# Four dense expert tiles on 512 columns instead of five on 640, and two tiles gathered early

## The chip, the cores and the metric

One Trainium2 chip, one of its cores. The metric is the device time of one execution in microseconds. Engines: PE is TensorE's matmul side, PEld its weight loads, DVE VectorE, ACT ScalarE, POOL GpSimd, SP SyncE, whose queue issues most transfers.

## The reference

One layer for a prompt of 1024 tokens and 32 sample rows (8 sequences of 4 tokens), all in float32:

```python
h = _rms(x, norm1_g) * (1.0 + sc1) + sh1
proj = h @ w_in
o_attn = _dilated_attn_prompt(q, k, v, rel_bias)        # or the same over a cache, for the sample rows
y_rwkv, s_fin, shift_new = _rwkv_mixer(proj[..., 3 * C_ATTN:], shift0, wkv0, ...)   # delta rule, a scan over time
x = x + g1 * (jnp.concatenate([o_attn, y_rwkv], axis=-1) @ w_out)
h2 = _rms(x, norm2_g) * (1.0 + sc2) + sh2
x = x + g2 * _peer(h2)

# _peer, per token: 8 heads, 16 of 16384 single-neuron experts each
s1, i1 = lax.top_k(s[:, :, 0], 16)
s2, i2 = lax.top_k(s[:, :, 1], 16)
top_s, pos = lax.top_k(cand, 16)                # cand: the 256 sums; eid: their experts
gate = jax.nn.softmax(top_s, axis=-1)
act = gelu(einsum('nd,nhkd->nhk', hb, expert_u[eid]))
out = einsum('nhk,nhkd->nd', gate * act, expert_v[eid])
```

So a token uses 128 of 16384 experts, each a row of expert_u and a row of expert_v of 1024 numbers.

## The kernel before, in words

The prompt is cut into eight tiles of 128 tokens, 0 to 7; the sample rows are tile NT. The expert sum of a tile is made in one of two ways.

*Gathered* (`gather_u`, `gather_v`, lines 1509 and 1524): for each of 128 picks POOL issues an indirect DMA that brings one row of expert_u for every token (128 rows of 4 KB into a tile `row`), DVE multiplies it with the token's h2 (held in two PSUM banks, `gh`) and sums; after Gelu and gate the same is done with expert_v, and DVE adds `row * co` to an accumulator in PSUM (`gh` or `ga`). Five `row` buffers go round (`NROW`), which also hold h2 and the operands of `finish`. A tile takes 256 gathers; the sample rows take 64.

*Dense* (`dense`, line 1615): all 16384 experts for the tokens of several tiles at once, in 128 blocks of 128 experts. `hidden(b)` loads u in two pieces of 256 KB, splits each into two float32r parts (ACT casts `uh`, POOL subtracts `ul`), and makes three products per block of channels into PSUM `d`; then ACT applies Gelu, DVE multiplies with the gates `g` loaded from DRAM, ACT and DVE split the product into `ch` and `cl`. `output` multiplies four blocks' `ch`, `cl` with `vh`, `vl` (v loaded and split likewise) and DVE adds the bank to `dacc`. The gates come from `spread_gates` (line 1553): per tile 256 small matmuls of one-hot factors (`oha` by POOL and ACT, `ohb` by DVE) into PSUM `sp`, copied to `stage` and written to `g_d` in four pieces of 2 MB.

Before the change tiles 0 to 4 are dense (640 columns, worked as two halves of 320) and tiles 5, 6, 7 and NT are gathered. The program has this order: norm, projection and the first two prompt quarters of the delta rule (`rwkv_prompt`), unchanged here; a front part (lines 1789 to 1875) with the last two quarters (`delta`), attention of tiles 2 to 5, the output projection and second norm (`front`), the routing scores (`scores`), the picks (`picks`, whose POOL instructions are `tq`) and the spreads (`spreads`), then sample rows and attention of tiles 6 and 7; then the dense experts, with the routing of tiles 6, 7 and NT (`routed`) and the gathers (`gather_all`) beside them.

`weave` puts such streams side by side: a rough meter of engine times decides which stream makes its next step, streams under `fill` only go along, and the others get a higher priority. The final order on each engine comes from the tile framework's scheduler when the program is built; on the chip each engine's queue runs strictly in that order and waits on semaphores. `until(x)` lets a stream idle until a tile is ready.

Of the kernel before, what the change touches and what calls it, by code (L numbers as in the profile page):

```python
# [11 lines left out]
FT = mybir.dt.float32  # L12
# [52 lines left out]
def _shape_constants():  # L65
# [20 lines left out]
    # relative bias along distance, from 1023 down  # L86
# [7 lines left out]
    # the sample rows' keys: 4 of every 16 far rows, the near ones, the new ones  # L94
# [35 lines left out]
class _Meter:  # L130
    """a rough count of the engines' time, by which streams of work are put side by side."""
# [43 lines left out]
class _Ring(dict):  # L175
    """tiles by number, made when first asked for."""
# [25 lines left out]
def tile_hybrid_step(ctx, tc, ins, outs):  # L202
# [27 lines left out]
    def split(src, hi, lo, eng=None):  # L230
        """src as a sum of two float32r parts."""
# [3 lines left out]
    def piece(pool, src, kn, eng, bufs, wbufs):  # L235
        """1024 columns of weights, of kn blocks of rows: as two float32r parts."""
# [6 lines left out]
    def mm3(out, l, r, first, last):  # L243
        """a product of split operands, to float32's accuracy; or of unsplit ones."""
# [9 lines left out]
    def rsqrt(pool, x, scale, bias, shape, name, floor=None):  # L254
        """1 / sqrt(scale * x + bias), with one Newton step behind the table."""
# [57 lines left out]
    def open_picked(es, name, tiles, ring=None):  # L313
        """the chosen experts of some tiles, and their gates."""
# [12 lines left out]
    def mod_rows(pool, seg, i, tag, n, bufs=1):  # L327
        """one of the six modulation vectors, a row for every token of tile i."""
# [16 lines left out]
    # ---------------------------------------------------------------- modulation, first norm  # L345
# [7 lines left out]
    def ada_rows(pa, pp, scT, r, bufs):  # L353
# [17 lines left out]
        if r == 2:  # L371
            # the second norm's weights times its scale
# [31 lines left out]
    def norm_rows(pa, tiles):  # L404
        """the rows of some tiles over their root mean square."""
# [16 lines left out]
    def norm_in(pa, pp, tiles, put):  # L422
        """first norm of some tiles, transposed: put(k, part) for the channels 128 k.. ."""
# [99 lines left out]
    # ---------------------------------------------------------------- the delta-rule heads  # L523
# [11 lines left out]
    def delta_consts(rc):  # L535
# [5 lines left out]
        # tiles that keep zeros where a block is empty  # L541
# [16 lines left out]
    def log_decay(pool, pp, lt, c0, n):  # L558
        """token-major logarithm of the decay."""
# [7 lines left out]
    def key_norms(pool, pp, sqk, n, nj):  # L567
        """1 / max(|kk|, 1e-12), token-major."""
# [8 lines left out]
    def spread(pool, pp, rn, p, n, nj):  # L577
        """the norms of a pair of heads over their columns, transposed."""
# [9 lines left out]
    def group_norm(pool, pp, y, n, bv, g, c0):  # L588
        """y token-major; normalised per head, the bonus and the gate put on, into columns c0.. of the mix."""
# [24 lines left out]
    def rwkv_prompt(pp, side, qs):  # L614
        """quarters of the prompt, 256 tokens each, in chunks of 64; heads go in two groups of four, side by side."""
        n = 256
        both = (0, 1)
        for qi in qs:
            t0 = 256 * qi
            with ExitStack() as es:  # L620
# [97 lines left out]
                with ExitStack() as e3:  # L718
# [14 lines left out]
                    # inverses of the 32-blocks: two partitions a block, for its even and its odd rows  # L733
# [30 lines left out]
                def chunk(j, gq, ych, py):  # L764
                    """two chunks of 64 tokens, four heads."""
# [41 lines left out]
                    # right-hand sides [A | M_ak V], then (I - M_ab)^-1 of them  # L807
# [1191 lines left out]
```

## Time and profile before

| | us |
|---|---|
| median of three runs | 3811.39 |
| lowest, highest | 3810.4, 3816.43 |
| span of the profiled execution, first to last instruction | 3802.4 |

The profiled execution's own time is given as its span; the runs' times also hold what lies before its first and after its last instruction. Busy shares of the span: PE 91%, DVE 76%, POOL 55%, ACT 38%. The kernel moves 981.58 MB. In the groups of rows below an instruction is named by output and inputs (`d<-h2T,uh`), buffer numbers left out; all carry line 196, the helper that records every operation, so they are told apart by their tiles. In the tables by window the columns are the window and its length, then busy time and instruction count of PE, PEld, DVE, ACT and POOL, then the granted TensorE clock, the mean busy share of the 16 DMA engines, and GB/s.

### The profile page before, as it was taken

The numbers are of one execution on the slowest core, as the hardware profiler recorded it, in microseconds if no ns is written. First come the engines' busy times: TensorE is split into PE (matmuls) and PEld (weight loads), VectorE is DVE, ScalarE is ACT, GpSimd is POOL, SyncE is SP. The second block draws the span as 40 slices with busy tenths as digits, with TensorE's granted clock in tenths as the row PEclk, the third lists the DMA queues.
The fourth block names the chain that finished last, engine by engine and source line by source line (L and its number), as shares of the span: only waits on it lengthen the run. The fifth ranks groups of instructions, "written<-read, shape, count | busy, mean of one in ns | idle before, by whom it ended". The sixth has DMA issues, their size and how long they took to land.

```text
span 3802.4 us, 57197 instructions
## 1 busy us (share of the span) xinstructions
PE 3473.4 (91%) x19618; PEld 2873.5 (76%) x19618; DVE 2899.8 (76%) x6059; ACT 1428.1 (38%) x3124; POOL 2107.3 (55%) x1842
## 2 busy tenths in 40 slices
PE   7999999789889888969999989999999999999998
PEld 3878678567768664547877879888887878788886
DVE  2655364588688566777878999888888888888898
ACT  5544344336766654542411322222222222222221
POOL 3232021015555356656655777677677767677775
PEclk8999999899999899989999999999999999999999
DMA  9643695553765667749988779999889898899998
GB/s 292 196 143 115 189 280 170 164 181 134 241 210 179 206 222 229 259 156 328 324 303 283 230 263 327 320 317 312 308 303 318 306 315 303 307 312 320 327 324 311
DMA packets 592528, 981.58 MB, mean 258 GB/s; under 512 B 78323, under 2 KB 354620, under 8 KB 589420
## 3 DMA queue, kind: packets, MB, share of 16 engines
q1 hardware_dynamic: 467788, 524.84, 43.1%
q0 software_dynamic: 124448, 453.08, 33.9%
q8 instruction: 155, 2.54, 0.3%
q14 instruction: 137, 1.12, 0.1%
HBM read 882.97 MB, written 94.78 MB: 257 GB/s over the span
## 4 chain that ended last, share of the span: by engine, by line
PE 36%; DVE 23%; DMA 19%; issue 11%; POOL 8%; ACT 3%; SPq 1%; POOLq 0%; DVEq 0%; ACTq 0%
PE at L196 10%; PE d L196 9%; DMA u<-in_uT 8%; PE rw L196 5%; PE pj L196 5%; POOL row L196 4%; PE rs L196 3%; DVE gh L196 3%; DVE act L196 2%; DVE row L196 2%; DVE cl L196 2%; PE sp L196 2%; DMA row<-in_expert_v,eid 2%; POOL vl L196 2%; POOL ul L196 2%
## 5 line engine op out<-in xcount | busy, mean ns | idle before, releaser
L196 PE MATMUL d<-h2T,uh 128*128 128x320 f32 x4096 | 908.1, 311 | 11.6 <-ACT h2T L196 7.0
L196 PEld LDWEIGHTS d<-h2T,uh 128*128 128x128 f32 x4096 | 689.7, 189 | 21.2 <-ACT h2T L196 7.3
L196 PE MATMUL d<-h2T,ul 128*128 128x320 f32 x2048 | 632.8, 310 | 0.3 <-POOL ul L196 0.3
L196 POOL DMA_INDIRECT row<-in_expert_u,eid x416 | 405.7, 975 | 264.3 <-DVE co L196 90.0
L196 PE MATMUL d<-vl,ch 128*128 128x512 f32 x1280 | 512.2, 401 | 43.6 <-POOL vl L196 43.6
L196 PE MATMUL d<-vh,ch 128*128 128x512 f32 x1280 | 486.4, 401 | 51.2 <-DVE dacc L196 26.9
L196 DVE CUSTOM_DVE_ANT_0 row<-row,gh 128x1024 f32<-128x1024 f32 x416 | 499.4, 1210 | 34.7 <-DMA row<-in_expert_u,eid 26.0
L196 POOL DMA_INDIRECT row<-in_expert_v,eid x416 | 406.4, 977 | 183.5 <-DVE gh L196 66.2
L196 PE MATMUL d<-vh,cl 128*128 128x512 f32 x1280 | 505.6, 396 | 0.8 <-DVE cl L196 0.7
L196 POOL TENSOR_SCALAR oha<-c_iota,tr 128x128 f32<-128x128 f32 x320 | 309.6, 974 | 310.8 <-PE sp L196 297.9
L196 POOL TENSOR_TENSOR ul<-u,uh 128x512 fp32r<-128x512 f32 x256 | 336.6, 1324 | 139.7 <-ACT uh L196 129.7
L196 ACT CAST vh<-v 128x512 fp32r<-128x512 f32 x256 | 157.5, 620 | 623.2 <-DMA v<-in_expert_v 447.9
L196 PEld LDWEIGHTS d<-h2T,ul 128*128 128x128 f32 x2048 | 386.2, 189 | 2.7 <-issue 1.6
L196 DVE SCALAR_TENSOR_TENSOR gh<-row,co,gh 128x1024 f32<-128x1024 f32 x285 | 364.9, 1280 | 27.7 <-DMA row<-in_expert_v,eid 26.0
L196 PEld LDWEIGHTS d<-vh,ch 128*128 128x128 f32 x1280 | 243.0, 191 | 129.8 <-DVE dacc L196 43.3
L196 DVE TENSOR_TENSOR act<-act,g 128x320 f32<-128x320 f32 x256 | 279.2, 1090 | 77.2 <-ACT act L196 72.8
L196 POOL TENSOR_TENSOR wl<-w,wh 128x1024 fp32r<-128x1024 f32 x50 | 122.5, 2453 | 388.7 <-ACT wh L196 353.9
L196 PEld LDWEIGHTS d<-vl,ch 128*128 128x128 f32 x1280 | 244.4, 191 | 112.0 <-POOL vl L196 62.1
L196 POOL TENSOR_TENSOR vl<-v,vh 128x512 fp32r<-128x512 f32 x224 | 289.5, 1301 | 34.7 <-ACT vh L196 30.3
L196 ACT CAST ch<-act 128x320 fp32r<-128x320 f32 x256 | 117.7, 460 | 495.4 <-DVE act L196 464.2
L196 PEld LDWEIGHTS d<-vh,cl 128*128 128x128 f32 x1280 | 244.9, 191 | 53.9 <-DVE cl L196 2.0
L196 ACT CAST uh<-u 128x512 fp32r<-128x512 f32 x256 | 154.0, 617 | 257.0 <-DMA u<-in_uT 166.2
(449 smaller groups left out, 6932.7 us busy)
## 6 DMA issues: line engine op xcount, KB each, us to landing
u<-in_uT SPq DMA_DIRECT2D x256, 256.0 KB
v<-in_expert_v SPq DMA_DIRECT2D x256, 256.0 KB
w<-wq_d SPq DMA_DIRECT2D x224, 256.0 KB
g_d<-stage SPq DMA_DIRECT2D x20, 2048.0 KB
g<-g_d SPq DMA_DIRECT2D x64, 640.0 KB
w<-in_w_in SPq DMA_DIRECT2D x75, 512.0 KB
w<-in_w_out SPq DMA_DIRECT2D x112, 256.0 KB
adaw<-in_ada_w SPq DMA_DIRECT2D x32, 512.0 KB
```

The lines of the kernel that those rows point to most:

```text
L196: return f(*a, **k)
```

## The change

Tiles 2 to 5 are dense, 512 columns in one piece; tiles 0 and 1 are gathered, from when they are picked. Gelu and product stay in the PSUM bank. The spreads of the four dense tiles move out of the delta-rule part into the part with the sample rows, where `rwkv_sample` and `attn_sample` now follow each other in one stream. `gather_all` goes along (`fill`) from the start of the front part. Attention of tiles 6 and 7 drops `wide` (second buffers of kT and vr). Removed comments are left out of the diff.

```diff
-    NDENSE = 640
+    NDENSE = 512
...
-            for h in range(2):
-                if b % 4 == 0:
-                    G_[h] = pa.tile([128, n // 64, 4, 32], FT, tag="g", name="g", bufs=3)
-                    sy.dma_start(G_[h], g_d[n // 64 * h:n // 64 * (h + 1), :, b:b + 4].rearrange("s e i t -> e s i t"))
-                cs = slice(h * n // 2, (h + 1) * n // 2)
-                ps = pp("d")
-                for k in range(KD):
-                    mm3(ps[:, :n // 2], (uh[:, k], ul[:, k]), [x[:, k, cs] for x in h2T], k == 0, k == KD - 1)
-                t = pa.tile([128, n // 2], FT, tag="act", name="act", bufs=2)
-                sc.activation(t, ps[:, :n // 2], AF.Gelu)
-                tv = t.rearrange("p (s t) -> p s t", t=32)
-                ve.tensor_tensor(tv, tv, G_[h][:, :, b % 4], op=OP.mult)
-                split(t, ch[:, cs], cl[:, cs])
+            if b % 4 == 0:
+                G_[0] = pa.tile([128, n // 32, 4, 32], FT, tag="g", name="g", bufs=2)
+                sy.dma_start(G_[0], g_d[:, :, b:b + 4].rearrange("s e i t -> e s i t"))
+            ps = pp("d")
+            for k in range(KD):
+                mm3(ps, (uh[:, k], ul[:, k]), [x[:, k] for x in h2T], k == 0, k == KD - 1)
+            sc.activation(ps, ps, AF.Gelu)
+            pv = ps.rearrange("p (s t) -> p s t", t=32)
+            ve.tensor_tensor(pv, pv, G_[0][:, :, b % 4], op=OP.mult)
+            split(ps, ch, cl)
...
-    dense_set = [0, 1, 2, 3, 4]
+    dense_set = [2, 3, 4, 5]
+    early_set = [0, 1]
+    front_set = early_set + dense_set
...
+    gat = open_pool(ctx, "gat")
+    pg = open_psum(ctx, "gatp", gh=1)
...
+    def gather_all():
+        for i in early_set:
+            yield from until(i)
+            yield from gather_u(gat, pg, i)
+            yield from gather_v(gat, bank_g, i)
+        yield from until(NT)
+        yield from gather_sample(gat, pg, bank_g)
+        yield from until("all")
+        yield from gather_u(gat, pg, 6)
+        yield from weave((gather_v(gat, bank_a, 6), False), (gather_u(gat, pg, 7), False))
+        yield from gather_v(gat, bank_g, 7)
+    some = gather_all()
...
-        streams = [front(), scores(), picks(), spreads()]
-        run(weave((delta(), True), fill=streams + [att]))
+        streams = [front(), scores(), picks()]
+        run(weave((delta(), True), fill=streams + [att, some]))
...
-                yield from attn_prompt(px, "left", [6, 7], wide=True)
+                yield from attn_prompt(p_at, "left", [6, 7])
...
+            streams.append(spreads())
             rest = weave(*((g, c) for g, c in zip(streams, (True, True, False, False))), (last(), True))
-            run(weave((rwkv_sample(lambda tag: other("rs"), "right"), True), (attn_sample(lambda tag: other("rs"), "right", pc), True), fill=[rest]))
-            run(rest)
+            run(weave((samples(), True), fill=[rest, some]))
+            run(weave((rest, False), fill=[some]))
...
-    def gather_all():
-        yield from gather_u(gat, pg, 5)
-        yield from gather_v(gat, bank_g, 5)
-        yield from until(NT)
...
```

Three places show what this does to POOL's queue. First, behind the first pick in the front part. Before (`tr_7962`, `neg` and `oha` belong to tile 0's spread, `moF` to the delta rule):

```order
L196 TENSOR_TENSOR tq<-td,te 128x800 x8
L196 TENSOR_SCALAR neg<-tr_7962 128x128 x2
L196 TENSOR_SCALAR oha<-c_iota_6639,tr_7962 128x128 x3
L196 TENSOR_TENSOR moF<-mab,c_mask_o 128x512
L196 TENSOR_SCALAR oha<-c_iota_6639,tr_7962 128x128 x2
L196 TENSOR_TENSOR moF<-mab,c_mask_o 128x512
L196 TENSOR_SCALAR oha<-c_iota_6639,tr_7962 128x128 x16
```

After (`eid_7561` are tile 0's picks; the second group of `tq` is tile 1's):

```order
L196 DMA row<-in_expert_u,eid_7561 128x1024
L196 TENSOR_TENSOR moF<-mab,c_mask_o 128x512
L196 DMA row<-in_expert_u,eid_7561 128x1024 x4
L196 TENSOR_TENSOR moF<-mab,c_mask_o 128x512
L196 DMA row<-in_expert_u,eid_7561 128x1024 x25
L196 TENSOR_TENSOR tq<-td,te 128x800 x2
L196 DMA row<-in_expert_u,eid_7561 128x1024 x4
L196 TENSOR_TENSOR tq<-td,te 128x800
```

Where the spread of tile 0 stood between the delta rule's instructions, gathers stand now. Second, beside the routing of tiles 6, 7 and NT. Before (`eid_13951` is tile 5):

```order
L196 TENSOR_TENSOR tq<-td,te 128x800 x2
L196 TENSOR_TENSOR ul<-u,uh 128x512
L196 DMA row<-in_expert_v,eid_13951 128x1024
L196 TENSOR_TENSOR ul<-u,uh 128x512
L196 DMA row<-in_expert_v,eid_13951 128x1024
L196 TENSOR_TENSOR tq<-td,te 128x800 x2
L196 DMA row<-in_expert_v,eid_13951 128x1024 x2
L196 TENSOR_TENSOR vl<-v,vh 128x512
```

After (`eid_8090` is tile 1, `eid_18813` the sample rows):

```order
L196 DMA row<-in_expert_v,eid_8090 128x1024
L196 TENSOR_TENSOR vl<-v,vh 128x512 x6
L196 TENSOR_TENSOR ul<-u,uh 128x512 x8
L196 TENSOR_TENSOR vl<-v,vh 128x512 x8
L196 TENSOR_TENSOR ul<-u,uh 128x512 x8
L196 TENSOR_TENSOR vl<-v,vh 128x512 x6
L196 TENSOR_TENSOR ul<-u,uh 128x512 x4
L196 TENSOR_TENSOR tq<-td,te 128x800 x2
...
L196 TENSOR_TENSOR ul<-u,uh 128x512 x2
L196 DMA row<-in_expert_u,eid_18813 128x1024 x5
```

The gathers of tile 5 that filled this stretch are gone; those of tile 1 end ahead of it, and the next ones follow the last pick. Third, the end of the queue. Before (`eid_18730` is tile 7):

```order
L196 DMA row<-in_expert_v,eid_18730 128x1024 x11
L196 TENSOR_TENSOR vl<-v,vh 128x512
L196 DMA row<-in_expert_v,eid_18730 128x1024
L196 TENSOR_TENSOR vl<-v,vh 128x512
L196 DMA row<-in_expert_v,eid_18730 128x1024
L196 TENSOR_TENSOR vl<-v,vh 128x512
L196 DMA row<-in_expert_v,eid_18730 128x1024
```

After (`eid_18446` is tile 7):

```order
L196 DMA row<-in_expert_v,eid_18446 128x1024 x5
L196 TENSOR_TENSOR vl<-v,vh 128x512 x2
L196 DMA row<-in_expert_v,eid_18446 128x1024 x2
L196 TENSOR_TENSOR vl<-v,vh 128x512
L196 DMA row<-in_expert_v,eid_18446 128x1024 x58
```

One gather stood behind the last `vl` and 58 stand there now. Over the whole queue there are 1088 gathers instead of 832: 231 ahead of the first `neg`, 235 from there to the first `ul`, 46 from there to the last `tq`, 518 from there to the last `vl`, and 58 behind it. Before, the first gather stood behind the first `ul`.

## Rows read from the trace of the kernel before

**Rows 1.** The page, its first line.
```profile
span 3802.4 us, 57197 instructions
```

**Rows 2.** Windows, by stage: PE, PEld, DVE, ACT, POOL busy (instructions), PEclk, DMA share, GB/s.
```profile
850.00:1294.00 444.00, 401.49 (x2527) 339.56 (x2526) 346.31 (x1293) 305.94 (x748) 230.65 (x223) 0.96 0.58 189
1294.00:1704.00 410.00, 341.34 (x1848) 210.24 (x1847) 283.15 (x806) 203.89 (x493) 239.92 (x175) 0.91 0.65 218
1704.00:2234.00 530.00, 511.08 (x2622) 414.44 (x2623) 446.93 (x1045) 143.79 (x270) 335.09 (x301) 0.98 0.85 290
2234.00:3756.00 1522.00, 1441.08 (x7872) 1281.57 (x7871) 1315.26 (x1620) 397.95 (x813) 1114.49 (x1018) 0.99 0.91 314
3756.00:3802.00 46.00, 28.35 (x122) 22.13 (x120) 40.28 (x50) 3.12 (x6) 15.40 (x13) 0.86 0.82 283
```

**Rows 3.** Tiles tq and vl: duration min/median/max, first to last start.
```profile
L196 POOL TENSOR_TENSOR tq<-td,te x66: 1522/1532/1971, 831.0 to 2233.0; 128x800 int32<-128x800 int32 x66
...
L196 POOL TENSOR_TENSOR vl<-v,vh x224: 1262/1298/1956, 1712.6 to 3778.4; 128x512 fp32r<-128x512 f32 x112
```

**Rows 4.** Timeline of PE: start us, us, engine, operation.
```profile
2519.64 0.39 PE L196 MATMUL d<-vh,ch 128*128 128x512 f32 x1
2519.86 0.39 PE L196 MATMUL d<-vl,ch 128*128 128x512 f32 x1
2520.09 0.39 PE L196 MATMUL d<-vh,cl 128*128 128x512 f32 x1
...
2521.00 0.46 PE L196 MATMUL d<-h2T,uh 128*128 128x320 f32 x2
2521.30 0.31 PE L196 MATMUL d<-h2T,ul 128*128 128x320 f32 x1
2521.44 0.46 PE L196 MATMUL d<-h2T,uh 128*128 128x320 f32 x2
```

**Rows 5.** Groups of instructions by form: count, busy us, mean ns, idle before and releasers.
```profile
L196 DVE CUSTOM_DVE_ANT_0 row<-row,gh 128x1024 f32<-128x1024 f32 x416 | 499.4, 1210 | 34.7 <-DMA row<-in_expert_u,eid 26.0 <-ACT gh L196 6.3 <-issue 0.9
...
L196 POOL DMA_INDIRECT row<-in_expert_v,eid x416 | 406.4, 977 | 183.5 <-DVE gh L196 66.2 <-issue 49.1 <-DVE co L196 36.6
...
L196 DVE SCALAR_TENSOR_TENSOR gh<-row,co,gh 128x1024 f32<-128x1024 f32 x285 | 364.9, 1280 | 27.7 <-DMA row<-in_expert_v,eid 26.0 <-DVE act L196 0.4
...
L196 POOL TENSOR_SCALAR oha<-c_iota,tr 128x128 f32<-128x128 f32 x320 | 309.6, 974 | 310.8 <-PE sp L196 297.9 <-PE at L196 5.5 <-ACT oha L196 4.1
...
L196 DVE TENSOR_TENSOR act<-act,g 128x320 f32<-128x320 f32 x256 | 279.2, 1090 | 77.2 <-ACT act L196 72.8 <-issue 2.8 <-ACT vh L196 0.9
...
L196 DVE TENSOR_TENSOR cl<-act,ch 128x320 fp32r<-128x320 f32 x256 | 215.0, 840 | 45.6 <-ACT ch L196 39.9 <-issue 4.7 <-ACT vh L196 0.8
L196 DVE TENSOR_TENSOR dacc<-dacc,d 128x512 f32<-128x512 f32 x310 | 204.2, 677 | 10.9 <-PE d L196 10.8
```

**Rows 6.** Windows again, of tile ohb alone: PE, PEld, DVE busy.
```profile
850.00:1294.00 444.00, 113.60 (x739) 104.30 (x740) 89.06 (x187) 0.96 0.58 189
1294.00:1704.00 410.00, 88.87 (x542) 77.21 (x542) 91.52 (x133) 0.91 0.65 218
```

**Rows 7.** The page: DMA issues, KB each.
```profile
g_d<-stage SPq DMA_DIRECT2D x20, 2048.0 KB
g<-g_d SPq DMA_DIRECT2D x64, 640.0 KB
```

**Rows 8.** Windows of 20 and 50 us, the fullest of the dense stage.
```profile
1900.00:1920.00 20.00, 20.00 (x115) 16.20 (x113) 16.58 (x27) 5.46 (x12) 13.69 (x13) 1.00 1.02 373
2600.00:2650.00 50.00, 47.74 (x257) 42.14 (x256) 44.44 (x70) 12.96 (x26) 39.02 (x37) 1.00 0.96 338
```

**Rows 9.** Groups of PE from 1704 to 2234 us.
```profile
L196 PE MATMUL d<-h2T,uh 128*128 128x320 f32 x852 | 195.2, 317 | 11.6 <-ACT h2T L196 7.0 <-ACT act L196 3.3 <-DVE h2T L196 1.3
...
L196 PE MATMUL d<-vl,ch 128*128 128x512 f32 x240 | 95.2, 398 | 0.0
```

**Rows 10.** Waits from 2250 to 3750 us: who for whom, us, times, longest.
```profile
ACT vh L196 <- DMA v<-in_expert_v: 383.9, 84, 11.1
```

More of the change, by code (lines that the diff above doesn't have):

```diff
@@ L1782, in until @@
             yield
-    open_picked(ctx, "picked_5", [5])
+    open_picked(ctx, "picked_E", early_set)
+    gat = open_pool(ctx, "gat")
+    pg = open_psum(ctx, "gatp", gh=1)
+    bank_g = lambda: pg("gh", D)
+    bank_a = lambda: banks("ga", D)
+    def gather_all():
[10 more added lines that the diff above has]
+    some = gather_all()
     h2_f = dram.tile([128, KD, NDENSE], FT, name="h2_f")
-    hcol = {i: 128 * i for i in dense_set}
+    hcol = {i: 128 * j for j, i in enumerate(dense_set)}
     with ExitStack() as es:
-        ps4 = open_psum(es, "frontp", at=3, sp=2)
-        p_at = lambda tag: ps4(tag if tag == "sp" else "at")
-        p_fr = lambda tag: ps4("at")
+        ps4 = open_psum(es, "frontp", at=3)
+        p_at = lambda tag: ps4("at")
         ed = ExitStack()
         pp = open_psum(ed, "deltap", rw=2, py=1)
-        open_picked(es, "picked_A", dense_set, 2)
-        ps_ = open_pool(es, "spread")
-        iota = load(ps_, "iota128")
-        stages = [lambda: ps_.tile([128, 128, 32], FT, tag="stage", name="stage", bufs=1)]
-        tops = open_tops(es, "tops_A", dense_set, ring=2)
+        open_picked(es, "picked_A", dense_set)
+        tops = open_tops(es, "tops_A", front_set, ring=2)
         pick = open_pick(es)
@@ L1822, in front @@
         def front():
-            for i in dense_set + [5]:
+            for i in front_set:
                 yield from until(("mix", i))
@@ L1826, in front @@
                     yield from until("q2")
-                yield from project_out(pf, p_fr, [i], new_x1, new_h2)
+                yield from project_out(pf, p_at, [i], new_x1, new_h2)
                 if i in hcol:
@@ L1832, in scores @@
         def scores():
-            for i in dense_set + [5]:
+            for i in front_set:
                 yield from until(("h2", i))
@@ L1836, in scores @@
                     yield from until(i - 2)
-                yield from route_scores(pf, p_fr, {i: h2A[i]}, tops)
+                yield from route_scores(pf, p_at, {i: h2A[i]}, tops)
                 ready.add(("scores", i))
@@ L1845, in picks @@
         def picks():
-            for i in dense_set + [5]:
+            for i in front_set:
                 yield from until(("scores", i))
@@ L1849, in picks, with spreads @@
                 ready.add(i)
-        def spreads():
-            for i in dense_set:
-                yield from until(i)
-                yield from spread_gates(ps_, p_at, i, 128 * i, iota, stages)
         ready.update((("mix", 0), ("mix", 1)))
         att = attention()
-        streams = [front(), scores(), picks(), spreads()]
-        run(weave((delta(), True), fill=streams + [att]))
+        streams = [front(), scores(), picks()]
+        run(weave((delta(), True), fill=streams + [att, some]))
         ed.close()
         er.close()
+        ps_ = open_pool(es, "spread", "right")
+        iota = load(ps_, "iota128")
+        stages = [lambda: ps_.tile([128, 128, 32], FT, tag="stage", name="stage", bufs=1)]
         with ExitStack() as e2:
-            other = open_psum(e2, "otherp", at=2, rs=1)
-            px = lambda tag: other("at")
+            other = open_psum(e2, "otherp", sp=2, rs=1)
+            def spreads():
+                for i in dense_set:
+                    yield from until(i)
+                    yield from spread_gates(ps_, other, i, hcol[i], iota, stages)
             def last():
@@ L1868, in last, with samples @@
                 ea.close()
-                yield from attn_prompt(px, "left", [6, 7], wide=True)
-            sample_consts(open_pool(e2, "sconst", "right"))
-            pc = open_pool(e2, "atts", "right")
+                yield from attn_prompt(p_at, "left", [6, 7])
+            def samples():
+                p_rs = lambda tag: other("rs")
+                sample_consts(open_pool(e2, "sconst", "right"))
+                yield from rwkv_sample(p_rs, "right")
+                yield from attn_sample(p_rs, "right")
+            streams.append(spreads())
             rest = weave(*((g, c) for g, c in zip(streams, (True, True, False, False))), (last(), True))
-            run(weave((rwkv_sample(lambda tag: other("rs"), "right"), True), (attn_sample(lambda tag: other("rs"), "right", pc), True), fill=[rest]))
-            run(rest)
+            run(weave((samples(), True), fill=[rest, some]))
+            run(weave((rest, False), fill=[some]))
     open_picked(ctx, "picked", [NT, 6, 7])
@@ L1904, in routed @@
                 ready.add(i)
-    pg = open_psum(ctx, "gatp", gh=1)
-    gat = open_pool(ctx, "gat", "right")
-    bank_g = lambda: pg("gh", D)
-    bank_a = lambda: banks("ga", D)
-    def gather_all():
-        yield from gather_u(gat, pg, 5)
-        yield from gather_v(gat, bank_g, 5)
-        yield from until(NT)
-        yield from gather_sample(gat, pg, bank_g)
-        yield from until("all")
-        yield from gather_u(gat, pg, 6)
-        yield from weave((gather_v(gat, bank_a, 6), False), (gather_u(gat, pg, 7), False))
-        yield from gather_v(gat, bank_g, 7)
-    some = gather_all()
     with ExitStack() as es:
```

## The prediction

> **What bounds the kernel now.** I cut the span of 3802.4 us [rows 1] at events that the change leaves in place or moves as a whole. Up to 850 us nothing can change: a gather needs picked experts, and POOL's first pick instruction (tq) starts at 831 us [rows 3]. Behind that stand four stages, and an end of 46 us [rows 2]: A, 850 to 1294, the last two prompt quarters of the delta rule beside three spreads; B, 1294 to 1704, sample rows, last attention, other spreads; C, 1704 to 2234, dense experts beside the routing of tiles 6, 7 and the sample rows (its last tq at 2233 [rows 3]); D, from there on, dense experts beside gathers.
>
> In those windows read PE's busy time against the stage's length, then DVE and POOL, then the DMA columns. PE has 511 of 530 us in C and 1441 of 1522 in D; the DMA engines are busy 0.91 of D at 314 GB/s, but only 0.58 and 0.65 of A and B, at 189 and 218 GB/s [rows 2]. So C and D are PE's, with DMA close behind, and A and B have DMA room. DMA is already more than a bystander: in the wait list ACT stands 384 us for v loads [rows 10]. The gathers themselves run freely: DVE waited only 26 us for gathered u rows in all [rows 5].
>
> **The change, part by part.**
>
> *Dense.* A dense matmul of 512 columns starts every 0.225 us, and three of 320 columns take 0.44 us [rows 4]. A block of 128 experts now needs 48 x 0.147 for hidden and 30 x 0.225 for output, 13.8 us; after, 24 x 0.225 and 24 x 0.225, 10.8 us. Over 128 blocks PE gets back 384 us.
>
> DVE's product and remainder now read two SBUF tiles at 1090 and 840 ns for 320 columns; afterwards they read PSUM, as dacc does at 677 ns for 512 [rows 5]. That is 256 x 1.93 = 494 us against 256 x 0.68 = 174. DVE bounds neither C nor D, so I credit no time to it. The bank is held longer instead, through Gelu, product, cast and remainder, about 2.6 us by DVE's 0.68 and as much on ACT. There are four banks, and three further outputs of 12 matmuls give PE 8 us before it comes round. I price this at 0; if DVE's queue holds four rows of 1.2 us ahead of the product, the cover is nearly used up, and my upper bound is 1 us a block, 128 us.
>
> *One more gathered tile.* 256 more gathers of 128 rows of 4 KB, 0.524 MB each: 134 MB. One spread less saves 4 writes of 2 MB, and the g loads fall from 64 x 640 KB to 32 of 1 MB [rows 7]: 17 MB together. Each gather also costs DVE 1.21 or 1.28 us and POOL 0.98 us [rows 5], to which I add 0.2 for the gap before the next one: 1.2 us on both.
>
> *Where they stand.* In POOL's order 231 gathers come before the first spread instruction, 235 more before the first ul. Only 46 stand beside the routing, 518 from there to the last vl, and 58 behind it.
>
> How fast can DMA go? D averages 314 GB/s; its fullest 50 us have 338, 20 us once 373 [rows 2, 8]. PE set the pace there, so 314 is no ceiling, but nothing sustained is above 338. I take the middle, 326, and keep 314 and 338 as bounds.
>
> Stage A. DVE: 346 us, less 89 for the moved ohb [rows 6], plus 231 x 1.2 = 534 us. DMA: 189 GB/s x 444 us = 84 MB, less three spreads (25), plus 121 = 180 MB, at 326 GB/s 552 us. PE's share shrinks and no longer matters. POOL's queue is strictly in order, so the delta rule's moF and the picks stand behind gathers that wait for one of five row buffers, and DVE, ACT and PE wait for them in turn. On SP's queue each early tile adds an h2 load and at its end the loads of finish, which wait for a row buffer with weight loads queued behind them, a few rows' time each. DVE at 0.95 busy gives 562 us; I take that (545 to 600).
>
> Stage B. DVE: 283, plus four spreads at 36 us instead of 91.5 (53), plus 235 x 1.2 = 618. POOL: 240, plus two spreads at 62 [rows 5] and 282 = 646. DMA: 89 MB, plus 17 for two more spreads, plus 123 = 229 MB, at 326 GB/s 702 us (678 to 730; with the in-order coupling of three nearly full engines up to 760). Attention of tiles 6 and 7 loses its second kT and vr buffers; its loads stand beside 700 us of other work, so that costs 0, or within the upper bound. So dense starts at 850 + 562 + 702 = 2114, where now it is 1704.
>
> Stage C. Now 852 + 426 hidden matmuls take 188 us, 720 outputs 162 [rows 9], and the routing the rest of PE's 511, 161. After, POOL places the last tq behind 52 ul, 26 blocks: 26 x 24 x 0.225 = 140, outputs 24 x 24 x 0.225 = 130, routing 161, sum 431; I take 435 (415 to 450). The DMA room here is now left empty, as 46 gathers replace nearly 200.
>
> Stage D, to the last vl, now at 3778 [rows 3]: 1544 us for 101 blocks. After, 102 blocks need PE 102 x 10.8 = 1102; POOL 382 instructions of 1.3 and 518 of 1.2, 1118; DMA 102 x 1.31 MB and 518 x 0.524, 405 MB, at 326 GB/s 1242 us. By today's share of PE, 101 x 13.8 / 1544 = 0.90, it would be 1221. I take 1242 (1199 to 1290).
>
> End. Today 24 us pass behind the last vl with one gather; 57 more at DVE's 1.28 us add 74 (70 to 87), with PE idle.
>
> Sum: 850 + 562 + 702 + 435 + 1242 + 24 + 74 = 3889 us of span. The shown median, 3811.4, is 9 us above the span of the profiled execution; with the same 9 I predict **3898 us**, 2.3% slower. All lower bounds give 3790, all upper ones 4070.
>
> Read the other way: behind 850 us the new kernel moves 819 MB (the sum of rate by length [rows 2]) + 117 = 936. Stage C takes about 71 of them in 435 us (26 blocks of 1.31 MB, 46 gathers, 12 MB of routing weights). To end at the old time the other 865 MB would have to pass in 2952 - 435 = 2517 us, 344 GB/s throughout. No 50 us of today's dense stage have that.
>
> **The rivals.**
>
> *DMA is no limit (faster).* The rate of D was only what PE asked for, and the gathers stream as in the best 20 us. Then A goes by DVE (545), B by POOL (646 / 0.97 = 666), C 415, D by PE at the 0.98 of stage C's first part (1102 / 0.97 = 1136), end 94: 3706, with the 9 3715 us. The point from which it decides is 344 GB/s. For it: the 373 of 20 us, and DVE's short waits for rows. Against: 384 us of waits for v, and that A and B need DVE or POOL almost without a gap. The Trainium skill, "DMA: Bandwidth & Descriptors", section Specifications, gives about 358 GB/s as what HBM yields a core; that rule speaks for this rival, and by it D's transfers would take 1131 us, less than PE. The trace exceeds it for 20 us and stays below it over 50 [rows 8]. Chance 0.13.
>
> *The front stretches further (slower).* Each gather ahead of a link of the chain (moF, tq, oha, attention's DVE work) delays it, and A and B run at 0.8 of their fullest engine: 534 / 0.8 + 646 / 0.8 = 1475 instead of 1264; 4109 us. For it: in A and B today no engine but PE is above 0.8. Against: gathers are work that fills gaps. Chance 0.2.
>
> *The longer held banks hit PE (slower).* 128 us more in C and D: 4026 us. Against: the 8 us of cover. Chance 0.1.
>
> *The front doesn't take the gathers, or each part gains as much as it loses (same).* It would need the order to be another than it is, or 344 GB/s to the point. Chance 0.04.
>
> **How the numbers follow.** The forecast itself has 0.53: DMA, DVE and POOL together, 3790 to 3990. Faster by over 0.2% (about what a measurement of this kernel can tell) only by the first rival: 0.13; same 0.04; slower 0.83. The range leaves out the faster rival's core and the far end of the stretched front: 3770 to 4050.
>
> **What would show it.** Right: first ul near 2114 us; the gather rate in A near 0.41 a us; DMA above 0.9 in A and B; a low DMA share for some 400 us behind the first ul; 58 gathers alone at the end with PE idle for 70 us; product and remainder at 0.68 us. Wrong: a first ul before 2050, 50-us stretches at 345 GB/s or more, or stage D near 1130 us.

## The result: 8.2% slower, beyond the range

The changed kernel takes 4128.7 us (median of 4 runs, 4108.6 to 4134.3), the kernel before 3813.9 beside it: ratio 1.0817, 95% interval 1.0787 to 1.0847. The forecast was 3898 us, with 3770 to 4050 as its range; the direction was right, the size was not.

The page of the changed kernel, its first line and two rows of DMA issues, stand against [rows 1, 7]:

```profile
span 4128.4 us, 49266 instructions
...
g_d<-stage SPq DMA_DIRECT2D x16, 2048.0 KB
g<-g_d SPq DMA_DIRECT2D x32, 1024.0 KB
```

The tiles tq and vl give the ends of stages C and D, as [rows 3] did:

```profile
L196 POOL TENSOR_TENSOR tq<-td,te x66: 1514/1532/1797, 836.6 to 2663.5; 128x800 int32<-128x800 int32 x66
...
L196 POOL TENSOR_TENSOR vl<-v,vh x224: 1260/1296/1827, 2259.9 to 4011.5; 128x512 fp32r<-128x512 f32 x112
```

Windows of the changed kernel by the prediction's stages (A, B, C, D, end), and a full one of 50 us. The columns are those of [rows 2]: stretch, length, PE, PEld, DVE, ACT, POOL busy, granted clock, DMA share, GB/s.

```profile
850.00:1443.00 593.00, 394.14 (x1858) 290.36 (x1859) 542.04 (x1509) 129.46 (x294) 268.70 (x260) 0.83 0.91 309
1443.00:2251.00 808.00, 488.27 (x2297) 309.80 (x2295) 614.70 (x1288) 341.01 (x801) 581.11 (x536) 0.78 0.81 286
2251.00:2664.00 413.00, 405.64 (x1724) 295.70 (x1724) 232.77 (x704) 114.32 (x195) 187.09 (x155) 0.99 0.55 186
2664.00:4012.00 1348.00, 1223.88 (x5030) 969.75 (x5029) 919.33 (x1262) 356.19 (x628) 995.91 (x908) 0.96 0.88 303
4012.00:4128.00 116.00, 4.19 (x19) 3.15 (x17) 93.10 (x80) 0.00 (x0) 56.52 (x59) 0.54 0.87 308
2150.00:2200.00 50.00, 25.93 (x57) 4.96 (x58) 32.87 (x27) 1.19 (x3) 24.99 (x27) 0.83 0.99 375
```

Read the lengths against the forecast first: A 593 (562), B 808 (702), C 413 (435), D 1348 (1242), end 116 (98). B and D are each 106 us over, A and the end 49 together, C gives 22 back: 239. The forecast had added 9 us for what lies around the span. That was mis-sized: the profiled execution of the changed kernel took 4130.1 us with a span of 4128.4, so 1.7 us lie around a span, and the rest of the 9 was the distance between two executions. The miss of the median is 231. Then multiply rate by length. B moved 231 MB and D 408 MB; the forecast had 229 and 405. The bytes were right, the rate of 326 GB/s was not.

Groups by form of the changed kernel, as in [rows 5] (count, busy us, mean ns, idle before and releasers):

```profile
L196 DVE CUSTOM_DVE_ANT_0 row<-row,gh 128x1024 f32<-128x1024 f32 x544 | 656.0, 1216 | 104.0 <-DMA row<-in_expert_u,eid 103.4
L196 DVE SCALAR_TENSOR_TENSOR gh<-row,co,gh 128x1024 f32<-128x1024 f32 x412 | 529.1, 1284 | 78.8 <-DMA row<-in_expert_v,eid 74.9
...
L196 DVE TENSOR_TENSOR d<-d,g 128x512 f32<-128x512 f32 x128 | 89.1, 697 | 94.2 <-ACT d L196 93.2
L196 DVE TENSOR_TENSOR cl<-d,ch 128x512 fp32r<-128x512 f32 x128 | 87.8, 687 | 120.9 <-ACT ch L196 120.6
...
L196 POOL DMA_INDIRECT row<-in_expert_u,eid x544 | 529.0, 972 | 301.9 <-DVE co L196 128.5 <-issue 60.7 <-DVE ga L196 24.7
```

Product and remainder take 0.70 and 0.69 us, against 0.68 forecast. But VectorE now waits 103 us for gathered u rows (544 gathers), where it waited 26 (416) [rows 5].

Two rows of the waits in stage D (2664 to 4012 us; who for whom, us, times, longest), and the longest stretch of loads on that stage's chain of waits (start, us, what; two u loads, one behind the other), show what PE lacked:

```profile
ACT vh L196 <- DMA v<-in_expert_v: 431.6, 109, 11.8
ACT uh L196 <- DMA u<-in_uT: 200.7, 51, 10.6
...
2752.57 19.87 DMA u<-in_uT x2
```

Before, the v row read 384 us [rows 10]; although the stage is shorter now, the wait has grown. In the grouped chain of this stage, u loads have 22.7% and PE's matmuls 20.9%.

### The profile page after: what moved, and what is told of

The parts are those of the page before. It is cut to its first block, busy times and chain, and to the rows that moved or that the text cites. A ratio compares the mean times of both kernels' runs of the same rounds, so it can differ in the third digit from the quotient of the medians.

```text
span 4128.4 us, 49266 instructions
## 1 busy us (share of the span) xinstructions
PE 3264.7 (79%) x15527; PEld 2470.4 (60%) x15527; DVE 2860.2 (69%) x6055; ACT 1316.0 (32%) x2711; POOL 2260.5 (55%) x2032
## 4 chain that ended last, share of the span: by engine, by line
PE 32%; DMA 29%; DVE 17%; issue 9%; POOL 8%; ACT 3%; SPq 1%; POOLq 0%; ACTq 0%; DVEq 0%
PE d L196 12%; DMA u<-in_uT 8%; PE at L196 7%; PE rw L196 4%; PE pj L196 4%; DMA row<-in_expert_v,eid 4%; POOL row L196 4%; DMA w<-wq_d 3%; DVE row L196 3%; POOL vl L196 2%; DMA w<-in_w_out 2%; PE rs L196 2%; DVE gh L196 2%; DMA cvt<-in_vc 2%; DMA v<-in_expert_v 2%
## 5 line engine op out<-in xcount | busy, mean ns | idle before, releaser
L196 DVE CUSTOM_DVE_ANT_0 row<-row,gh 128x1024 f32<-128x1024 f32 x544 | 656.0, 1216 | 104.0 <-DMA row<-in_expert_u,eid 103.4
L196 POOL DMA_INDIRECT row<-in_expert_u,eid x544 | 529.0, 972 | 301.9 <-DVE co L196 128.5
L196 PE MATMUL d<-h2T,uh 128*128 128x512 f32 x2048 | 648.7, 398 | 4.8 <-DVE dacc L196 4.8
L196 DVE SCALAR_TENSOR_TENSOR gh<-row,co,gh 128x1024 f32<-128x1024 f32 x412 | 529.1, 1284 | 78.8 <-DMA row<-in_expert_v,eid 74.9
L196 PEld LDWEIGHTS d<-h2T,uh 128*128 128x128 f32 x2048 | 386.9, 189 | 102.7 <-DVE dacc L196 6.1
L196 PE MATMUL d<-h2T,ul 128*128 128x512 f32 x1024 | 407.5, 398 | 1.9 <-POOL ul L196 1.9
L196 PE MATMUL at<-w,h2A 128*128 128x256 f32 x768 | 231.6, 440 | 79.5 <-DMA w<-wq_d 72.7
L196 PE MATMUL sp<-oha,ohb 128*128 128x128 f32 x1024 | 190.7, 331 | 114.9 <-issue 37.6
L196 PEld LDWEIGHTS sp<-oha,ohb 128*128 128x128 f32 x1024 | 164.0, 231 | 167.4 <-issue 63.8
L196 PE MATMUL at<-w,m 128*128 128x256 f32 (+1 forms) x576 | 175.4, 446 | 95.8 <-DMA w<-in_w_out 91.3
```

Source lines behind the costliest of these rows:

```text
L196: return f(*a, **k)
```

## The experiments

"Changed" below is the changed kernel. Where a run left work out, the expectation says which. Where no number of runs is given, a time is that of one profiled run; the kernel before took 3803 to 3816 us beside them, and the four times of the changed kernel spread over 26 us.

**1. No gathers at all.** `gathered(...)` and VectorE's work on its rows are left out, both sums set to 0.

> The changed kernel without any gather: no row of expert_u or expert_v is brought in for tiles 0, 1, 6, 7 and the sample rows, and DVE's work on them is left out, so their expert sum is zero. Stages by the same events as before: A 850 to the first neg, B to the first ul, C to the last tq, D to the last vl. Theory 1 (the gathers, by DMA and DVE, set the pace of A, B and D): A falls from 593 to 400-450 us, B from 808 to 430-520, D from 1347 to 1110-1170 (102 blocks of 10.8 us), the span to 2.9-3.05 ms. Rival (the moved spreads and the sample rows in one stream make B long by themselves): B stays above 650 us. Rival for D (banks held through the product, PE waits whatever the gathers do): D stays above 1250 us.

3448.2 us. Windows of stages A to D, whose ends are the same events:

```profile
850.00:1303.00 453.00, 370.86 (x2021) 284.15 (x2021) 317.26 (x1345) 142.61 (x315) 61.23 (x41) 0.93 0.52 156
1303.00:1859.00 556.00, 413.58 (x2142) 272.88 (x2141) 298.37 (x726) 323.16 (x779) 344.22 (x293) 0.85 0.52 178
1859.00:2239.00 380.00, 370.50 (x1562) 265.75 (x1562) 179.63 (x660) 106.74 (x180) 128.57 (x96) 0.99 0.42 134
2239.00:3426.00 1187.00, 1187.00 (x5161) 968.65 (x5160) 316.00 (x464) 370.10 (x640) 514.06 (x402) 1.00 0.38 117
```

The last tq comes at 2239 us, where it came before the change (2233 [rows 3]). So by that mark the 512 gathers of tiles 0 and 1 cost the front 425 us, 0.83 us each. The rest of the new order is not free, though: without one gather B takes 556 us, where it took 410 [rows 2]. C hides that, with 380 us instead of 530, because its blocks are shorter, 23 of them pass instead of 27, and tile 5's gathers no longer stand in it. In D, PE is busy without a gap, although ScalarE waits there too:

```profile
ACT vh L196 <- DMA v<-in_expert_v: 296.5, 146, 5.8
```

That stage began at block 23 (46 of 256 ul had passed), so 1187 us for 105 blocks is 11.3 us a block: PE's own pace, against the 10.8 that I took from its starts. A, B and D came 3, 36 and 17 us above what I had expected; the span expected, 2.9 to 3.05 ms, was a slip, as the expected stages with the 850 us ahead of them and C come to some 3.2 to 3.4 ms.

**2. More buffers for the dense loads.**

```
-u ... tag="u", bufs=3      -v ... tag="v", bufs=2
+u ... tag="u", bufs=6      +v ... tag="v", bufs=4
```

> The changed kernel with 6 buffers for u and 4 for v instead of 3 and 2. Theory 1 (in D the DMA engines' bandwidth, some 300 GB/s beside the gathers, is the limit): D stays within 40 us of 1347. Rival (the loads of u are issued too late, each group of four blocks waits 10 to 15 us for one): D falls by 100 to 240 us, to 1110-1250, and the span to 3.9-4.03 ms.

4007.2 us. Stage D and the end, in windows:

```profile
2683.00:3821.00 1138.00, 1134.35 (x4920) 922.80 (x4919) 860.67 (x1200) 357.67 (x618) 941.60 (x855) 1.00 0.95 335
3821.00:4005.00 184.00, 9.08 (x41) 7.18 (x39) 154.71 (x131) 0.00 (x0) 101.97 (x105) 0.53 0.89 321
```

D falls by 210 us to PE's pace (1134 of 1138 us busy), while the DMA engines move 335 GB/s on average. The 326 GB/s that I let carry stage D were no ceiling; loads asked for too late were. 68 us go back at the end: 104 gathers, not 58, now stand behind the last vl. D and the end together took 1464 us in changed and take 1322 here, less than the 1340 forecast for them.

**3. The sample rows' two parts side by side again.** `samples()` is taken apart, so that the two run as streams of their own, as before the change; `oha` and `ohb` get 2 buffers instead of 3.

> The changed kernel with the delta rule and the attention of the sample rows as two streams side by side again, as before the change (two buffers for the one-hot factors instead of three, to make room). Theory 1 (B is full of gathers and spreads): B stays within 40 us of 808. Rival (attention of the sample rows, left for the end of B, is a chain of cache loads with little beside it, 143 us behind the last spread): B falls by 80 to 150 us and the span to about 4.0 ms.

4111.2 us. Stages B and C:

```profile
1436.00:2099.00 663.00, 438.62 (x2045) 284.16 (x2045) 535.77 (x1166) 284.63 (x646) 484.41 (x431) 0.75 0.86 296
2099.00:2652.00 553.00, 474.60 (x1939) 346.27 (x1939) 322.86 (x815) 178.32 (x343) 282.99 (x258) 0.86 0.59 197
```

The first ul comes 152 us earlier, the last tq 12. So B fell by 145 us, as the rival had it, but the time did not follow: what left B came back in C. The last spread's matmuls, 71 us of PE, now run behind the first ul, and C has 93 gathers instead of 46 (B 187 instead of 235):

```profile
1436.00:2099.00 663.00, 175.12 (x796) 144.31 (x797) 57.17 (x101) 0.75 0.86 296
2099.00:2652.00 553.00, 70.97 (x239) 54.24 (x238) 17.39 (x30) 0.86 0.59 197
```

These are the same windows for the spread's tile `sp` alone (PE, PEld, ACT; in changed all of it lies in B). The serial sample chain makes B long, but it is not what the front as a whole lost.

**4. Only the product in PSUM, in the kernel before** (five dense tiles).

```
-t = pa.tile([128, n // 2], FT, tag="act", ...); sc.activation(t, ps[:, :n // 2], AF.Gelu)
+t = ps[:, :n // 2];                             sc.activation(t, t, AF.Gelu)
```

> The kernel before with one part of the change alone: Gelu and product stay in the PSUM bank (two halves of 320 columns, five dense tiles). Theory 1 (DVE bounds neither C nor D, PE and DMA do): within 0.7% of the kernel before, 3785-3840 us, though product and remainder fall from about 1090 and 840 ns to under 600. Rival (the stretched product delays the chain to ch and cl and the release of row buffers): 40 to 100 us faster. Rival (longer held banks): 40 to 130 us slower.

3766.9 us against 3815.6: ratio 0.9878 (0.9854 to 0.9902). This part alone makes the kernel faster, by 1.2%, which is the first rival's 40 to 100 us and not theory 1; product and remainder take 0.50 and 0.49 us. Its D is 1479 us for 99 blocks (before 1545 for 101), and ScalarE still waits 371 us for v loads there.

**5, 6. The front's gathers without VectorE's work, and the reverse.**

```
5:  gathered(...) stays; its tensor_tensor_reduce / scalar_tensor_tensor left out for tiles 0, 1
6:  row = one constant tile; the 512 VectorE operations stay, gathered(...) left out for tiles 0, 1
```

> Tiles 0 and 1: their 512 gathers are issued as in the changed kernel, but VectorE doesn't work on the rows (no dots, no weighted sum; the two sums are set to 0). Read the time of the last tq, 2664 us in the changed kernel and 2239 us without any gather. Theory 'transfers' (weight, query and cache loads of the front arrive late behind the gathered rows): the last tq stays above 2500 us. Theory 'VectorE' (each gather's 1.2 to 1.3 us of VectorE work delays the links of the chain): the last tq falls below 2350 us.

> The reverse: the VectorE work for the 512 gathers of tiles 0 and 1 stays (on one constant row, into the same row buffers), the gathers themselves are left out, and with them their place in GpSimd's queue and their transfers. Theory 'transfers': the last tq near that without any gather, below 2350 us. Theory 'VectorE': above 2500 us. If both this run and the one with gathers alone lie in the middle (2350 to 2500 us), the two costs add.

Last tq at 2556 us with gathers alone (4014.5 us in all) and at 2663 with VectorE's work alone (4149.4 us; changed 2664, neither 2239). Both theories lose: each half alone brings most of the delay or all of it, and the two don't add. Stages A and B of run 5:

```profile
850.00:1342.00 492.00, 304.75 (x1518) 229.74 (x1517) 239.35 (x871) 116.94 (x275) 234.57 (x229) 0.78 0.84 303
1342.00:2099.00 757.00, 528.05 (x2657) 355.96 (x2657) 411.21 (x1188) 341.65 (x804) 577.86 (x524) 0.83 0.90 316
```

A is 492 us there with 206 of its 231 gathers, 39 above the 453 without any; with VectorE's work beside them it is 593. Stages A and B of run 6 show how VectorE does it:

```profile
850.00:1756.00 906.00, 545.71 (x2512) 400.32 (x2512) 868.21 (x2423) 171.69 (x396) 87.64 (x56) 0.79 0.34 107
1756.00:2293.00 537.00, 363.21 (x1928) 239.48 (x1928) 306.46 (x534) 314.68 (x766) 342.07 (x285) 0.79 0.46 160
```

With no transfer to wait for, the work went ahead into A, where VectorE was busy 868 of 906 us and what else VectorE had to do stood behind it in its queue. As work moved between the stages (in run 5 91 gathers stand in C, not 46), these two runs don't tell B's causes apart; 12 to 14 do.

**7. More weight buffers in the front:** `NW = 3` became `NW = 5`.

> The changed kernel with five buffers instead of three for the weights of the output projection and of the routing in the front part. Theory 'transfers', in the form that a load is asked for too late because its buffer comes free late: the last tq comes 50 to 150 us before 2664 us. Theory 'VectorE', or transfers that are limited by their rate: within 25 us of 2664 us.

The last tq comes at 2684 us, 20 later, and the time is 4184.4 us. Late weight buffers aren't what holds the front, as far as this run tells: its A also took 32 more gathers. The 56 us by which it is slower lie mostly behind it: C took no gathers (46 in changed), and D, with 523, took 1389.

**8. The product in PSUM and a ring, in the kernel before.** Experiment 4 and one ring for both dense loads:

```
-u ... tag="u", bufs=3     -v ... tag="v", bufs=2
+u ... tag="u", bufs=7     +v ... tag="u", bufs=7
```

> The kernel before (five dense tiles) with Gelu and product in PSUM as in the fourth experiment, and with one ring of seven buffers for the dense u and v loads instead of three and two. If the late u and v loads were what held the dense stage there too (371 + 194 us of ScalarE's waits), stage D goes from 1479 us to PE's pace: 1428 us busy or a little less, 1400 to 1440, and the time from 3767 us to 3700 to 3730 us. If the rate of the transfers holds it (324 GB/s in that stage), it stays within 15 us of 3767 us.

The tiles `g2` and `fx` of the last steps go round in the same ring. 3699.9 us (5 runs) against 3813.0: ratio 0.9701 (0.9676 to 0.9726), the fastest kernel here that leaves no work out, with five dense tiles. Its stage D:

```profile
2254.00:3665.00 1411.00, 1402.91 (x7837) 1275.73 (x7836) 1138.97 (x1616) 397.67 (x804) 1075.85 (x1003) 1.00 0.95 335
```

PE is busy for 1403 of 1411 us. So late loads held the dense stage before the change too, and cost the kernel of experiment 4 67 us (3766.9 to 3699.9; in this stage 1479 us for 99 blocks to 1411 for 98). The 371 us of ScalarE's waits there were not their price.

**9, 10. Only the v loads (4 buffers), only the u loads (6).**

> The changed kernel with four buffers instead of two for the dense v loads; the u loads keep three. In the second experiment both were raised and stage D (last tq to last vl) went from 1348 to 1138 us, 104 gathers then standing behind the last vl. ScalarE's waits name v (432 us of stage D) before u (201 us), the chain of waits names u (22.7%) before v (5.6%). If the waits are right, stage D falls to 1250 us or less; if the chain is right, it stays above 1290 us.

> The changed kernel with six buffers instead of three for the dense u loads; the v loads keep two. If the chain of waits is right (u), stage D falls to 1250 us or less; if ScalarE's waits are right (v), it stays above 1290 us. If each alone gives about half of the 210 us, the loads wait for one another on SyncE's one queue.

4071.2 and 4027.3 us. Stage D of the first, then of the second:

```profile
2658.00:3894.00 1236.00, 1185.64 (x5014) 948.15 (x5013) 912.75 (x1220) 359.67 (x628) 959.24 (x869) 0.98 0.89 314
```

```profile
2677.00:3894.00 1217.00, 1173.23 (x4960) 938.00 (x4961) 904.19 (x1245) 356.11 (x623) 977.81 (x891) 0.98 0.92 329
```

D falls by 112 and 131 of the 210 us: about half each, as expected if the loads wait for one another on SyncE's one queue; that a load whose buffer is not free holds those behind it is argued from the queue's order, not shown. But part of the fall is gathers that moved behind the last vl (96 and 71 stand there, not 58). With the end counted in, the v buffers gain 53 us, the u buffers 116 and both 142, and the times say the same (58, 101 and 122 us). So the chain, which put u first, was a better guide than the longest row of the wait list, as far as single runs tell.

**11. Product and remainder in SBUF, on 512 columns.** `t = pa.tile([128, n], ..., bufs=2)` takes Gelu's result.

> The changed kernel with Gelu's result, product and cast in an SBUF tile of 512 columns, so that the PSUM bank is free after Gelu. If the longer held bank is part of what stage D lost (up to 128 us), stage D falls below 1290 us and the time below 4090 us. If it is not, VectorE's product and remainder take over 1.2 us each instead of 0.70 and 0.69 us, and stage D stays at 1348 us or grows by up to 60 us.

4182.8 us, D 1378. VectorE's groups from 2700 to 4000 us, in D (columns as above):

```profile
L196 DVE TENSOR_TENSOR hact<-hact,g 128x512 f32<-128x512 f32 x98 | 162.4, 1657 | 33.2 <-ACT hact L196 33.2
L196 DVE TENSOR_TENSOR cl<-hact,ch 128x512 fp32r<-128x512 f32 x98 | 146.5, 1495 | 143.8 <-ACT ch L196 143.7
```

Freeing the bank earlier gains nothing that outweighs 1.66 and 1.50 us in place of 0.70 and 0.69. As the run changes both, it doesn't rule the longer held bank out by itself; experiments 1, 2 and 15 do, in which PE runs D with hardly a gap, the banks held as in changed.

Why the product is slow in SBUF its spread shows (min/median/max in ns, here and, second, in D of changed):

```profile
L196 DVE TENSOR_TENSOR hact<-hact,g x98: 676/1640/3503, 2701.6 to 3984.8; 128x512 f32<-128x512 f32 x98
L196 DVE TENSOR_TENSOR d<-d,g x104: 685/697/700, 2665.2 to 3997.0; 128x512 f32<-128x512 f32 x104
```

Two of them on the timeline of experiment 11, the first beside a gather, the second beside GpSimd's subtraction for `ul`:

```profile
3010.67 0.95 POOL L196 DMA_INDIRECT row<-in_expert_u,eid  x1
3010.72 0.69 DVE L196 TENSOR_TENSOR hact<-hact,g 128x512 f32<-128x512 f32 x1 [2.29 <-ACT hact L196]
...
3016.83 1.31 POOL L196 TENSOR_TENSOR ul<-u,uh 128x512 fp32r<-128x512 f32 x1
3016.95 1.75 DVE L196 TENSOR_TENSOR hact<-hact,g 128x512 f32<-128x512 f32 x1
```

Of the 98, the 30 that no GpSimd subtraction overlapped took 0.68 us on average and at most 0.74; the 68 others took 2.09 us, each about its overlap and 0.5 to 0.9 us more.

**12. Tile 1 not gathered.**

> The changed kernel, tile 1 not gathered at all (its sum is set to 0), so 256 gathers of the front part remain, 231 of them in stage A as before and 25 in B instead of 235. If each early gather delays the front by the same amount (425 us for 512, 0.83 us each), the last tq comes at 2450 us. If stage B is set by what its gathers add to engines and transfers, A stays at 593 us, B falls from 808 to under 620 us. If B is held by the sample rows' serial chain instead, B stays above 720 us.

3910.6 us, last tq at 2420 us (2450 if every gather cost the same): the first 256 early gathers cost 181 us, the second 256 cost 244. Stages A and B:

```profile
850.00:1437.00 587.00, 407.09 (x1852) 301.66 (x1851) 538.27 (x1494) 128.26 (x290) 266.16 (x257) 0.80 0.91 309
1437.00:2050.00 613.00, 446.98 (x2298) 301.50 (x2296) 371.25 (x956) 331.71 (x796) 389.77 (x326) 0.83 0.58 199
```

A is the changed kernel's; B is 613 us, so its 210 further gathers cost 195 us.

**13, 14. Tile 1's gathers without VectorE's work, and the reverse,** edited as in 5 and 6, for tile 1 alone.

> The changed kernel; for tile 1 the gathers stay, VectorE doesn't work on their rows (sum set to 0). Stage A as before (225 gathers, within 15 us of 593). If the transfers delay stage B, B stays above 750 us (808 in the changed kernel with 235 gathers, 613 with 25). If VectorE's work does, B falls to 640 us or less.

> The reverse for tile 1: VectorE's 256 operations stay, on one constant row, its gathers are left out (25 gathers of tile 0 are left in B). Some of that work may move ahead into stage A, so A and B are read together: 1401 us in the changed kernel, 1200 without tile 1. If the transfers delay the front, A + B is 1250 us or less; if VectorE's work does, 1350 us or more; about 1300 us if both do in part.

4088.4 and 4015.8 us. Stage B with tile 1's gathers alone (251 of them here, 235 in changed), then with its VectorE work alone (A is 591 and 583 us in them):

```profile
1441.00:2222.00 781.00, 482.09 (x2283) 312.03 (x2282) 393.25 (x944) 340.19 (x798) 598.49 (x553) 0.76 0.87 306
```

```profile
1433.00:2149.00 716.00, 460.87 (x2301) 310.19 (x2300) 656.48 (x1341) 338.33 (x800) 373.42 (x327) 0.78 0.50 171
```

From 613 us the gathers alone go to 781, VectorE's work alone to 716 (VectorE busy 0.92 of it), both together to 808. Last tq comes at 2637 and 2527 us (one tile alone 2420, changed 2664), and A and B together take 1299 us in run 14, the value expected if both halves count. The gathers carry more of B's delay, and VectorE's work covers much of the same time. "Gathers" here are their transfers and their places in GpSimd's queue together; these two weren't separated.

**15. A ring of ten for u and v, in the changed kernel.**

> The changed kernel with one ring of ten buffers for the dense u and v loads. If late loads are all that stage D lost against PE's pace (1138 us with six and four buffers), D again takes 1130 to 1160 us and the time is 3990 to 4020 us; stages A to C don't change (last tq within 25 us of 2664 us). If the second experiment's time was one lucky execution, it lies above 4050 us.

4018.7 us (4 runs), ratio to before 1.0562 (1.0531 to 1.0593). Stage D:

```profile
2693.00:3827.00 1134.00, 1132.93 (x4916) 922.05 (x4915) 860.04 (x1197) 356.64 (x618) 936.95 (x851) 1.00 0.95 335
```

PE is busy for 1133 of 1134 us, as in experiment 2, and ScalarE's waits for v are down to 24 us. The last tq came 29 us later than in changed, just outside the 25 expected. 110 us of the 315 are won back; 107 gathers stand behind the last vl.

## Why the prediction was off, point by point

**Up to stage A: right.** A was costed by VectorE at 0.95 busy; it was 0.91 and 593 us, inside 545 to 600. Experiment 5 bears that out: without VectorE's work on the rows A took 492 us. The gather rate was 0.39 a us (231 in 593; 0.41 forecast), the DMA share 0.91.

**Stage B: the step "229 MB, at 326 GB/s 702 us" failed,** and its bound of 760 with it. With the gathers alone B ran at 306 GB/s and took 781 us; with VectorE's work as well, 286 and 808. The transfers do come out as B's largest part, but at a rate below stage D's of before; that this is because they share the stretch with chains that wait in order is argued from the shares, which leave no engine full: DMA 0.81, VectorE 0.76, GpSimd 0.72. The rival "the front stretches further" had B at 646 / 0.8 = 808, which is what B took. To the us that is luck: GpSimd was busy for 581 us, not 646 (its forecast held the gaps), and the fullest engine, VectorE, for 0.76. That engines in order leave gaps was right for B; its A (534 / 0.8 = 668) was too long. Its chance of 0.2 was too low for B. Why I missed it: I took each engine's sum for a bound and the in-order coupling for an addition of 30 to 58 us, though experiment 1 shows that without a single gather A and B take 453 and 556 us with no engine above 0.82. I also took B's 410 us of before as the base, to which only bytes and engine time were added. The new order alone made it 556, 25 gathers 613 (experiment 12), all of them 808. Of that order, the dropped second buffers of kT and vr, put at 0, were never run by themselves. What the lower clock cost wasn't separated either: the spread's matmuls took 331 ns in B at a granted 0.78, 296 before at 0.91. Which link of B waits for which row is still not settled.

**Stage C: right.** 413 us, 2 below the range of 415 to 450, with PE busy for 406 of them; DMA share 0.55, as foreseen.

**Stage D: the step "DMA 405 MB, at 326 GB/s 1242 us" failed.** It was a wrong limit, not only a wrong size: the rate is what the late loads left, 303 GB/s, and with deeper buffers the same engines ran at 335 for 1138 us (experiments 2 and 15). PE's bound beside it was too low as well: 102 blocks at 11.3 us are 1153, not 1102. I had read ScalarE's 384 us of waits for v [rows 10] as DMA standing close behind PE. They were a latency: a block of dense work shrank from 15.3 to 13.2 us (1545 us for 101 blocks, 1348 for 102), the buffers stayed at three and two, and beside the gathers the chain shows up to 16 us of waiting for one u load and 20 for two in a row; without gathers the same buffers let PE run without a gap (experiment 1). The row alone could not have priced this: ScalarE's waits for v stood at 297 us with PE never idle (experiment 1), at 371 with 67 us lost (experiments 4 and 8) and at 432 with 142 lost (D and the end, experiment 2). It should have kept me from taking the bytes as the limit; a run with deeper buffers would have told.

The 326 itself rested on a misreading. The two windows of [rows 8] are not the fullest of the dense stage; the kernel before had a fuller one, which by itself refutes "no 50 us of today's dense stage have" 344 GB/s, and another of 345 GB/s in stage D, from 3580 us:

```profile
1870.00:1920.00 50.00, 50.00 (x295) 43.08 (x294) 41.46 (x74) 20.76 (x43) 34.65 (x33) 1.00 0.98 350
```

So "50-us stretches at 345 GB/s or more", one of the signs of being wrong, could not tell: the kernel before had them, and the changed one has 375 GB/s in B.

**End: mis-sized.** 58 gathers as forecast, but 1.70 us apart (first at 4015.5, last at 4112.5), not VectorE's 1.28, so the 74 us (57 x 1.28 is 73) were 97. VectorE waits for rows in between, at a DMA share of 0.87. Whether the rate of the transfers or the round of only five `row` buffers sets the 1.70 us is not separated: 0.524 MB in 1.70 us are 308 GB/s either way.

**The rivals.** "DMA is no limit" needed 344 GB/s throughout. Stage D could have had PE's pace, as that rival said (1136 us, which is 1102 / 0.97 and not the 0.98 of its sentence), but with buffers that neither kernel has; in no run with the whole early work did the front end near this rival's 2476 us (850 + 545 + 666 + 415). On the page that I set beside it: the Trainium skill, "HBM Reference", section Specifications (TRN2), says that a core streaming alone measures well above the per-core share of about 358 GB/s; the trace agrees, with 375 GB/s over 50 us at a DMA share of 0.99. "The longer held banks hit PE" falls with experiments 1, 2 and 15, where PE has hardly a gap in D, and with product and remainder at 0.70 and 0.69 us. "Same" had nothing for it. One term that I put at nothing was worth something: product and remainder in PSUM, credited with no time, bring the kernel before 49 us (experiment 4).

**What the change traded.** Without gathers the span is 3446 us (experiment 1). The early gathers cost the front 425 us, D is 161 longer with its gathers (1348 for 102 blocks, not 1187 for 105), and the last of them add 97 at the end: 3446 + 683 = 4129. Of the change's parts the product in PSUM is worth 49 us to the kernel before (3815.6 to 3766.9); with the ring, which is no part of the change, it is 113.

## What to carry to other kernels

When a stage's work per block shrinks, count the loads in flight, not only the bytes: buffers that just suffice may not do when blocks come sooner beside a fuller DMA. A row of waits for loads warns of that, but it is no price; one run with deeper buffers gives the price. Before work is moved beside a chain, take the chain's own utilisation (here no engine above 0.82 with nothing beside it) as the sign that engines in order won't be filled to 0.95. A change that bundles several edits can hide a good one; time the parts apart.

## What the runs showed of the hardware

- VectorE's product on 512 columns with both inputs in SBUF took 0.68 us where no GpSimd subtraction ran beside it and 2.09 on average where one did (experiment 11); with one input in PSUM it took 0.685 to 0.700 us in stage D, whatever GpSimd did. A gather on GpSimd did not lengthen it. The Trainium skill, "SBUF — State Buffer", section "Who interferes with whom", has a VectorE instruction with two SBUF inputs contend with a GpSimd instruction that reads SBUF, and one with a single SBUF input not; the durations agree.
- The DMA engines held 335 GB/s for 1134 to 1411 us beside a full PE in three kernels (experiments 2, 8, 15), close to the 338 that I had kept as the upper bound; the best 50 us of experiment 2's stage D had 363.
- The granted TensorE clock fell to 0.83 in A and 0.78 in B, means over stretches at 1.2 and 2.4 GHz, where PE was busy 0.66 and 0.60 of the time; before, it was 0.96 and 0.91, with PE busy 0.90 and 0.83 [rows 2]. In C and D it came back to 0.99 and 0.96.
